# A hybrid encoder step on one core: which groups of the down projection use seven products, and where the first weights stand among the input's pieces

## The chip, the core and the metric

The kernel runs on one core of one Trainium2 chip. The time is device microseconds of one execution of the whole program. The kernel before took 2386.49 us, the median of 3 runs (2385.48 to 2387.06). One more execution was profiled: it took 2391.23 us, and its trace spans 2389.5 us from the first instruction to the last. All places below are microseconds from the start of that span.

Engine names: PE is the matrix engine (TensorE), PEld its weight loads, DVE the vector engine (VectorE), ACT the scalar engine (ScalarE), POOL is GpSimd, SP the engine whose queue issues every transfer of this kernel.

## The reference, cut to what matters

One layer of a streaming encoder, 2048 prompt tokens and 64 tokens of a running stream, model width 1024, all in float32:

```python
h = rmsnorm(x, norm1_w)
proj = h @ w_in                      # 1024 -> 2568 columns
# (A) q, k, v: causal convolution of width 4 + SiLU, gated delta rule in chunks (4 heads x 128)
# (B) 512 columns: trailing means over 2/4/8/16 frames, a 128x128 map per group, a scale
x = x + jnp.concatenate([o_delta, o_pool], axis=-1) @ w_out
h = rmsnorm(x, norm2_w)
x = x + (jax.nn.silu(h @ w_gate) * (h @ w_up)) @ w_down     # 1024 -> 2816 -> 1024
y = rmsnorm(x, normf_w)
```

It returns y for both streams and the new convolution, delta and pooling states. The change concerns the last product, `@ w_down`, and the first transfers of the program.

## The kernel before, in words

**Numbers as pairs.** Nearly every large float32 product is done on pairs: an operand is split into a high part (ACT copies it to the `F32R` type) and a low part (DVE subtracts the high part from the original). A product of two pairs is three matmuls (high·high, high·low, low·high). A split therefore costs one ACT and one DVE instruction, for weights and for activations.

**First stage** (0 to about 996 us): the tokens, 2112 in all, go through in four blocks. Block 0 takes its input as the tile pair `x0` (lines 459 and 478 to 481): two token halves (`S0`, 288 tokens each), each loaded by four transfers of two 128-row slices. `norm_apply` (line 754) turns slices into pairs, k = 0 to 7 for one half and then for the other; behind k = 1 of the first half it calls `prep()` (line 775), which loads and splits the first weight tile of `w_in` (two transfers of 256 KB). Ahead of it stand `WARM` = 12 matmuls of ones (lines 466 and 467).

**FFN stage** (from 996 us): three blocks b = 0, 1, 2 of 704 tokens, each in two halves of N2 = 352. The 2816 hidden columns are 22 tiles f of 128. For each f, `gate_up` (line 1498) makes gate and up at once in seven products of half-size operands (Strassen's scheme, 84 matmuls of 128x352); its result lies in one of three buffers `hr`. In block 0 the seven weight combinations of a tile are made by POOL, split by ACT and DVE and stored to memory (`prep_strassen`, line 577); blocks 1 and 2 load the finished pairs back.

The down projection takes the f in `FGROUPS` = (4, 4, 2, 4, 4, 4), six groups numbered 0 to 5. Group 0 follows gate/up tile 5, and groups 1 to 5 follow tiles 8, 10, 14, 18 and 21. A group is done in one of two ways:

- *plain* (`down`, line 1544): for each of 8 output tiles m and each token half, 3G matmuls, and one DVE addition of the sum in PSUM to `y`. Weights: 8 tiles of G·128 columns, each one transfer, one ACT and one DVE instruction. The activations are pairs per f and half.
- *in seven products* (`down_strassen`, line 1584): for each of 4 pairs of output tiles, 7 products of 3G/2 matmuls, each followed by a DVE addition to `y`. Weights (`prep_down`, line 611): per pair of output tiles two transfers, four POOL combinations, and four splits. The activations, two f at a time, are combined and split in `factors` (line 1561): four POOL instructions and seven splits.

Which way is set by `SDOWN` = (1, 2) (line 48) and `plain` (line 503): in block 0 all six groups are plain; in blocks 1 and 2 all are in seven products but for group 5 of block 2. The pairs of block 0 are written by `finish` (line 1516) into six places `h3t` (two tiles of three, line 1602); those of blocks 1 and 2 into tiles of the same two buffers (tag `op`), two f in each.

**What sets the order.** The program is written down in one order, and `Machine` (line 59) collects the instructions with their dependences. `issue` then writes each engine's instructions by a list planner: it keeps a modelled time per engine (costs in `cost`, line 140), and takes among the ready instructions that of the lowest rank, which is the place in the written order less a boost (`BOOST`, `HURRY`). Buffers are handed out in the plan too: an instruction whose tile has no free buffer isn't ready. On the chip each engine works through its list in order. Weight tiles are prepared up to four entries of `plan` ahead (`weights_ahead`, line 632), within the buffers: four of `wsp`, four of `wsp2` for pairs, four of `wraw` and three of `wraw2` for raw weights.

Of the kernel before, what the change touches and what calls it, by code (L numbers as in the profile page):

```python
# [12 lines left out]
F32R = mybir.dt.float32r  # L13
# [5 lines left out]
P = 128  # L19
D = 1024  # L20
KT = D // P
# [19 lines left out]
TB2 = NTOK // NB2  # L41
N2 = TB2 // 2
# [2 lines left out]
SUBS2 = ((0, N2), (N2, N2))  # L45
FGROUPS = (4, 4, 2, 4, 4, 4)

SDOWN = (1, 2)

FW = ("11", "S1", "S2", "12", "S3", "S4", "22")  # L50
FH = ("11", "T1", "T2", "21", "T3", "22", "T4")
# [302 lines left out]
def hybrid_kernel(ctx, tc, a, o):  # L354
    nc = machine = Machine(tc.nc)
# [120 lines left out]
    nw = cpool.tile([P, 3 * KT], F32, tag="nw", name="nw")  # L476
    nc.sync.dma_start(out=nw, in_=a["nw"])
    for lo, n in S0:
        for i in range(0, KT, 2):
            nc.sync.dma_start(out=x0[i // 4][:, i % 4 : i % 4 + 2, lo : lo + n],  # L480
                              in_=a["xT"][i : i + 2, :, lo : lo + n].rearrange("k p t -> p k t"))
    n1w, n2w, nfw = (nw[:, i * KT : (i + 1) * KT] for i in range(3))


# [14 lines left out]
    def halves(b, gi):  # L499

        return ((0,), (1,)) if (b, gi) == (NB2 - 1, len(groups) - 1) else ((0, 1),)

    def plain(b, gi):
        return b not in SDOWN or len(halves(b, gi)) > 1

    order = []
    for b in range(NB2):
# [246 lines left out]
    def norm_apply(B):  # L754

        hh = [bp.tile([P, 4, 2, MB], F32R, tag=f"h{i}", name=f"h{i}_{B.j}") for i in range(2)]
        B.h = [(k, hh[k // 4][:, k % 4]) for k in range(KT)]
        src = stream_x(a["xT"], "xb", B.t0)
        machine.boost = BOOST
        for lo, n in S0 if B.j == 0 else [(0, B.NB)]:  # L760
            sl = slice(lo, lo + n)
            for k in range(KT):
                w, h = n1w[:, k : k + 1], B.h[k][1]
                if B.j == 0:
                    t = from_x0(k, lo, n)
                    act(h[:, 0, sl], t, AF.Copy, scale=w)
                    stt(h[:, 1, sl], t, w, h[:, 0, sl].bitcast(F32), ALU.mult, ALU.subtract)
                else:
                    t = src(k, lo, n)
                    stt(t, t, w, B.r[:, sl], ALU.mult, ALU.mult)  # L770
                    split(h, sl, t)
                if B.j == lo == 0 and k == 1:

                    machine.boost = 2 * BOOST
                    prep()
                    machine.boost = BOOST
        machine.boost = 0
# [720 lines left out]
    def gate_up(b, f):  # L1498
# [17 lines left out]
        def finish(i, g, u):  # L1516
            e = raw[:, i]
            tt(e, e, g, ALU.mult)
            tt(e, e, u, ALU.mult)
            if b not in SDOWN:  # L1520
                split(h3t[f % 6], slice(i * N2, (i + 1) * N2), e)


        x, y, z = (psg(f"p{i}_{tag}")[:, :N2] for i in "xyz")
# [14 lines left out]
        finish(1, g2, u2)  # L1539
        add(x, "22", "T4")  # L1540
        finish(0, g1, x)
        return raw if b in SDOWN else h3t[f % 6]

    def down(b, gi, h3, ys, which, done):
        f0, G = groups[gi]
# [68 lines left out]
    for op in order:  # L1614
        b = op[1]
        if op[0] == "gu":
# [3 lines left out]
            if op == ("gu", 0, 2):  # L1620
                nxt = Chain(between(-1))
            h3[f] = gate_up(b, f)
            if b in SDOWN:
                gi = max(g for g, (f0, G) in enumerate(groups) if f0 <= f)
                if plain(b, gi):
                    if f == groups[gi][0] or f == groups[gi][0] + 2:
                        two = opool.tile([P, 2, 2, TB2], F32R, tag="op", name=f"h3l{f}", bufs=2)
                    for i in range(2):
                        split(two[:, f % 2], slice(i * N2, (i + 1) * N2), h3[f][:, i])
                    h3[f] = two[:, f % 2]  # L1630
                elif f % 2:
                    h3[f] = factors(b, f, h3.pop(f - 1), h3[f])
# [19 lines left out]


AHEAD = 3
WARM = 12
PSM = 3
BOOST = 100000

# [133 lines left out]
```

## Time and profile before

| | |
|---|---|
| median of 3 runs | 2386.49 us (2385.48 to 2387.06) |
| the profiled execution | 2391.23 us, span 2389.5 us |
| PE busy | 2347.9 us, 98% of the span, 14803 matmuls recorded |
| DVE, ACT, POOL busy | 70%, 51%, 41% of the span |
| first stage | 0 to 996 us |
| FFN block 0, 1, 2 | 996 to 1463, to 1920, to the end |

The profile's page gives the span and each engine's busy time. Matmuls are pipelined, so their recorded durations overlap: what counts is the time from one start to the next. The view of windows gives busy times, instruction counts, the granted PE clock and the rate of the transfers for any stretch; an instruction that straddles an edge is counted, and a few per cent of matmul records can be missing. In the groups of instructions a row reads: engine, operation, output<-inputs by the program's names (wsd, wsdS: pairs of the down weights; wrd, wrdt, wrdl, wrda, wrdb: raw ones; hq, h7: activations of the seven products; d and dx, dy, dz: PSUM sums of a plain group and of the seven products), shapes, count | busy us, mean ns of one | idle time ahead of it, and who ended that.

### The profile page before, as it was taken

The page shows a single profiled execution, that of the slowest core. Times are in us where ns is not written, and L with a number is a line of the kernel's source. Part 1 is how long each engine was busy: PE and PEld are TensorE (multiplying, and loading weights), DVE is VectorE, ACT ScalarE, POOL GpSimd, SP SyncE. Part 2 cuts the span into 40 slices and gives each one's busy share as a digit, 9 for nine tenths or more (in the row PEclk, how much of TensorE's full clock was granted, in tenths as well). Part 3 has the DMA queues.
Part 4 walks back from the last instruction along what each step waited for, and adds up shares of the span by engine and source line. Part 5 has one row for each costly group of instructions (what it writes and reads, how often), then busy time and mean ns, then how long its engine had stood idle before and what let it go on. Part 6 is the DMA issues. An engine that isn't in the chain of part 4 may idle for free.

```text
span 2389.5 us, 41681 instructions
## 1 busy us (share of the span) xinstructions
PE 2347.9 (98%) x14803; PEld 2183.0 (91%) x14803; DVE 1681.2 (70%) x2963; ACT 1217.8 (51%) x2746; POOL 971.1 (41%) x1146
## 2 busy tenths in 40 slices
PE   9999999999999999999999999999999999999998
PEld 8999798778887878899999999999899999999998
DVE  7999875785577786787776763767566657666466
ACT  6666654564456464574454554553333554434334
POOL 1656442554356652264332226454233464222111
PEclk9999999999999999999999999999999999999999
DMA  7644566455555575999876778976755697566763
GB/s 267 224 166 137 184 224 220 143 168 189 177 184 177 165 192 171 320 370 338 294 284 225 280 264 260 309 260 238 278 192 178 199 350 247 174 211 210 260 207 115
DMA packets 228448, 540.57 MB, mean 226 GB/s; under 512 B 28304, under 2 KB 86672, under 8 KB 228240
## 3 DMA queue, kind: packets, MB, share of 16 engines
q1 hardware_dynamic: 228240, 537.92, 66.8%
q8 instruction: 116, 1.90, 0.3%
q14 instruction: 92, 0.75, 0.1%
HBM read 389.41 MB, written 148.41 MB: 225 GB/s over the span
## 4 chain that ended last, share of the span: by engine, by line
PE 83%; DVE 8%; ACT 3%; DMA 2%; issue 2%; POOL 1%; SPq 0%; DVEq 0%; POOLq 0%; ACTq 0%
PE px L278 19%; PE pp L278 14%; PE pz L278 12%; PE py L278 10%; PE d L278 8%; PE dx L278 6%; PE dy L278 3%; PE pk_p L278 2%; PE pt_p L278 1%; PE dz L278 1%; PE gr_p L278 1%; DVE y L278 1%; PE px_p L278 1%; DVE Yqk L278 1%; PE py_p L278 1%
## 5 line engine op out<-in xcount | busy, mean ns | idle before, releaser
L278 PE MATMUL pp<-h,wsp 128*128 128x512 f32 (+1 forms) x2480 | 562.1, 366 | 3.9 <-DVE h L278 2.8
L278 PEld LDWEIGHTS pp<-h,wsp 128*128 128x128 f32 x2480 | 402.6, 190 | 52.0 <-DVE h L278 3.9
L278 POOL TENSOR_TENSOR Um_p<-Gst_p,lmask 128x256 f16<-128x256 f32 x224 | 179.0, 813 | 108.1 <-PE py_p L278 79.3
L278 PE MATMUL pz<-op,wsp 128*128 128x512 f32 (+1 forms) x960 | 216.7, 366 | 2.5 <-ACT op L278 2.0
L278 PEld LDWEIGHTS pz<-op,wsp 128*128 128x128 f32 x960 | 155.8, 190 | 22.5 <-ACT op L278 2.5
L278 PE MATMUL d<-h,wsd 128*128 128x352 f32 x1056 | 169.6, 322 | 0.0
L278 PEld LDWEIGHTS d<-h,wsd 128*128 128x128 f32 x1056 | 168.3, 188 | 0.5 <-DVE h L278 0.5
L278 DVE TENSOR_TENSOR TV_p<-TV_p,pt_p 128x512 f16<-128x512 f16 (+1 forms) x192 | 128.5, 681 | 48.4 <-PE pt_p L278 43.1
L278 PE MATMUL px<-hA,ws 128*128 128x352 f32 x792 | 141.9, 324 | 0.3 <-DMA ws<-g 0.3
L278 PE MATMUL pz<-hB,ws 128*128 128x352 f32 x792 | 139.9, 322 | 0.3 <-DMA ws<-g 0.3
L278 PE MATMUL py<-hB,wsS 128*128 128x352 f32 x792 | 139.1, 322 | 0.3 <-ACT u L278 0.3
L278 PE MATMUL px<-hBT,wsS 128*128 128x352 f32 x792 | 137.6, 322 | 1.9 <-ACT g L278 1.9
L278 PE MATMUL px<-hBT,ws 128*128 128x352 f32 x792 | 137.9, 322 | 1.5 <-DVE u L278 1.5
L278 PE MATMUL px<-hA,wsS 128*128 128x352 f32 x792 | 137.4, 322 | 0.9 <-ACT g L278 0.9
L278 POOL TENSOR_TENSOR wrS<-wr,wrS 128x512 f32<-128x512 f32 x44 | 62.9, 1430 | 185.4 <-DMA wrS<-in_wu_dram 61.2
L278 PE MATMUL py<-hA,wsS 128*128 128x352 f32 x792 | 137.4, 322 | 0.0
L278 ACT ACTIVATE hr<-g 128x352 f32<-128x352 f32 x132 | 65.7, 498 | 132.3 <-DVE g L278 131.9
L278 PEld LDWEIGHTS px<-hBT,wsS 128*128 128x128 f32 x792 | 128.2, 188 | 2.5 <-ACT g L278 2.5
L278 PEld LDWEIGHTS px<-hA,ws 128*128 128x128 f32 x792 | 129.8, 189 | 0.7 <-DMA ws<-g 0.6
L278 PEld LDWEIGHTS px<-hBT,ws 128*128 128x128 f32 x792 | 128.0, 188 | 2.3 <-DVE u L278 2.1
L278 PEld LDWEIGHTS px<-hA,wsS 128*128 128x128 f32 x792 | 128.3, 188 | 1.2 <-ACT g L278 1.2
L278 PEld LDWEIGHTS pz<-hB,ws 128*128 128x128 f32 x792 | 128.7, 188 | 0.6 <-issue 0.6
(690 smaller groups left out, 5499.8 us busy)
## 6 DMA issues: line engine op xcount, KB each, us to landing
wsS<-gS SPq DMA_DIRECT2D x176, 512.0 KB, 4.7
ws<-g SPq DMA_DIRECT2D x132, 512.0 KB, 4.7
wsp<-wnd SPq DMA_DIRECT2D x126, 512.0 KB, 3.5
gS<-wsS SPq DMA_DIRECT2D x88, 512.0 KB, 5.3
g<-ws SPq DMA_DIRECT2D x66, 512.0 KB, 5.3
wnd<-wsp SPq DMA_DIRECT2D x42, 512.0 KB, 4.7
xd<-x2d SPq DMA_DIRECT2D x96, 176.0 KB, 4.0
wrd<-in_wd_dram SPq DMA_DIRECT2D x56, 256.0 KB, 4.3
```

The source lines that it names most:

```text
L278: getattr(getattr(self.nc, op.eng), name)(*args, **kw)
```

## The change

`SDOWN` goes; a list `PLAIN` of (block, group) says which groups are plain. In block 0, group 4 (tiles 14 to 17) is now done in seven products. In blocks 1 and 2, group 2 (tiles 8 and 9) is now plain. Group 5 of block 2 stays plain through `halves`. The six places `h3t` go: in every block the pairs of a plain group are now split behind `gate_up`, into tiles of two f from the two `op` buffers, as blocks 1 and 2 did for their plain group.

At the start `x0` comes in four transfers of four slices instead of eight of two, `prep()` for the first weights is called behind k = 3 instead of k = 1, and `WARM` is 22 instead of 12.

```diff
-SDOWN = (1, 2)
+PLAIN = ((0, 0), (0, 1), (0, 2), (0, 3), (0, 5), (1, 2), (2, 2))
...
     for lo, n in S0:
-        for i in range(0, KT, 2):
-            nc.sync.dma_start(out=x0[i // 4][:, i % 4 : i % 4 + 2, lo : lo + n],
-                              in_=a["xT"][i : i + 2, :, lo : lo + n].rearrange("k p t -> p k t"))
+        for i in range(2):
+            nc.sync.dma_start(out=x0[i][:, :, lo : lo + n],
+                              in_=a["xT"][4 * i : 4 * i + 4, :, lo : lo + n].rearrange("k p t -> p k t"))
...
     def plain(b, gi):
-        return b not in SDOWN or len(halves(b, gi)) > 1
+        return (b, gi) in PLAIN or len(halves(b, gi)) > 1
...
-                if B.j == lo == 0 and k == 1:
+                if B.j == lo == 0 and k == 3:
                     machine.boost = 2 * BOOST
                     prep()
...
             tt(e, e, g, ALU.mult)
             tt(e, e, u, ALU.mult)
-            if b not in SDOWN:
-                split(h3t[f % 6], slice(i * N2, (i + 1) * N2), e)
...
-        return raw if b in SDOWN else h3t[f % 6]
+        return raw
...
-    six = [opool.tile([P, 3, 2, TB2], F32R, tag="op", name=f"h3_{i}", bufs=2) for i in range(2)]
-    h3t = [six[i // 3][:, i % 3] for i in range(6)]
...
             h3[f] = gate_up(b, f)
-            if b in SDOWN:
-                gi = max(g for g, (f0, G) in enumerate(groups) if f0 <= f)
-                if plain(b, gi):
...
+            gi = max(g for g, (f0, G) in enumerate(groups) if f0 <= f)
+            if plain(b, gi):
+                if f == groups[gi][0] or f == groups[gi][0] + 2:
+                    two = opool.tile([P, 2, 2, TB2], F32R, tag="op", name=f"h3l{f}_{b}", bufs=2)
+                for i in range(2):
+                    split(two[:, f % 2], slice(i * N2, (i + 1) * N2), h3[f][:, i])
+                h3[f] = two[:, f % 2]
+            elif f % 2:
+                h3[f] = factors(b, f, h3.pop(f - 1), h3[f])
...
-WARM = 12
+WARM = 22
```

More of the change, by code (lines that the diff above doesn't have):

```diff
@@ L1622, in hybrid_kernel @@
             h3[f] = gate_up(b, f)
-            if b in SDOWN:
-                gi = max(g for g, (f0, G) in enumerate(groups) if f0 <= f)
-                if plain(b, gi):
[L1626 to L1632, printed above, removed]
+            gi = max(g for g, (f0, G) in enumerate(groups) if f0 <= f)
[7 more added lines that the diff above has]
+                h3[f] = factors(b, f, h3.pop(f - 1), h3[f])
             if f == NF - 1 and b + 1 < NB2:
```

## The prediction, made before the changed kernel was run

> **What bounds the kernel now.** First the page: its span, and the busy time of each engine.
>
> ```profile
> span 2389.5 us, 41681 instructions
> ## 1 busy us (share of the span) xinstructions
> PE 2347.9 (98%) x14803; PEld 2183.0 (91%) x14803; DVE 1681.2 (70%) x2963; ACT 1217.8 (51%) x2746; POOL 971.1 (41%) x1146
> ```
>
> PE is busy all along, so only two things can move the end: fewer or shorter matmuls, and the places where PE waits. The profiled execution took 2391.23 us, 1.7 us more than its span; the sum below is made against it and carried over to the median, 2386.49 us. Next the view of windows, for the five kinds of down group and for the gate/up tiles around the group that changes in block 0. The columns: stretch, length, then busy time (instructions) of PE, PEld, DVE, ACT and POOL, the granted clock, and the transfers.
>
> ```profile
> 1208.02:1223.52 15.50, 15.50 (x99) 15.50 (x98) 15.26 (x27) 5.46 (x10) 5.83 (x4) 1.00 0.49 175
> 1361.12:1391.83 30.71, 30.71 (x195) 30.71 (x194) 17.34 (x28) 6.22 (x11) 8.31 (x6) 1.00 0.40 148
> 1744.42:1771.64 27.22, 27.22 (x172) 27.22 (x171) 19.62 (x39) 5.62 (x11) 8.69 (x10) 1.00 0.53 166
> 1669.60:1691.67 22.07, 18.84 (x95) 14.96 (x95) 19.87 (x42) 4.46 (x12) 8.52 (x12) 1.00 0.62 204
> 2127.34:2148.59 21.25, 19.39 (x101) 17.30 (x100) 18.57 (x40) 4.51 (x12) 6.14 (x10) 0.92 0.59 193
> 1307.54:1361.12 53.58, 53.58 (x339) 53.58 (x338) 38.27 (x60) 34.78 (x70) 14.05 (x10) 1.00 0.83 310
> 1391.67:1431.86 40.19, 40.19 (x255) 40.19 (x254) 27.73 (x44) 26.57 (x54) 9.65 (x7) 1.00 0.88 317
> ```
>
> The first three rows are dense. Group 2 of block 0, plain, is 96 matmuls (8 tiles, 2 halves, 6 each) in 15.50 us, and group 4, plain, 192 in 30.71 us: 0.160 us each. Row three, a group of four in seven products in block 1, holds 172 records less two that straddle its edges: 170 times 0.160 is 27.2 us, the row's length, so nothing is lost there. Rows four and five are the groups of two in seven products, in blocks 1 and 2. They hold 95 and 101 records, without the edges 93 and 99, that is 14.9 and 15.8 us of matmuls in 22.07 and 21.25 us. So 7.2 and 5.4 us are lost. In both, DVE is busy nearly throughout (19.87 and 18.57 us). What PE waits for there stands in the view of waits, around the one group and around the other (total, times, longest; the longest rows):
>
> ```profile
> PE px L278 <- DVE u L278: 1.1, 1, 1.1
> PE dx L278 <- DVE wsdS L278: 0.8, 1, 0.8
> ```
>
> ```profile
> PE dx L278 <- DVE y L278: 0.9, 1, 0.9
> ```
>
> All of it is DVE. The first, 1.1 us, falls at the end of gate/up tile 10, ahead of row four's stretch, while DVE already splits the group's first weights.
>
> **Blocks 1 and 2: the group of two becomes plain.** The groups of DVE instructions give the reason for the loss: mean ns is the number ahead of the second bar.
>
> ```profile
> L278 DVE TENSOR_TENSOR y<-y,dx 128x352 f32<-128x352 f32 x176 | 88.7, 516 | 33.9 <-PE dx L278 33.3
> L278 DVE TENSOR_TENSOR wsd<-wrdt,wsd 128x256 fp32r<-128x256 f32 x8 | 6.5, 812 | 0.0
> L278 DVE TENSOR_TENSOR wsdS<-wrda,wsdS 128x256 fp32r<-128x256 f32 x8 | 4.5, 559 | 0.0
> L278 DVE TENSOR_TENSOR wsdS<-wrdb,wsdS 128x256 fp32r<-128x256 f32 x8 | 3.6, 451 | 0.0
> L278 DVE TENSOR_TENSOR wsd<-wrdl,wsd 128x128 fp32r<-128x128 f32 x8 | 4.0, 506 | 0.0
> L278 DVE TENSOR_TENSOR wsd<-wrd,wsd 128x256 fp32r<-128x256 f32 x8 | 3.4, 421 | 2.3 <-DMA wr<-in_wg_dram 1.5 <-ACT wsd L278 0.9
> ```
>
> In seven products a group of two asks DVE for 28 additions of 0.516 us (14.4 us) and four times the four splits (0.812 + 0.559 + 0.451 + 0.506 = 2.33, in all 9.3 us): 23.7 us, for 84 matmuls of 13.4 us. Plain it asks for 16 additions (8.3 us) and 8 splits of 0.421 us (3.4 us): 11.7 us, for 96 matmuls of 15.4 us. PE becomes the bound again. The 16 POOL combinations of its weights and four of its activations go, and seven activation splits become four. The bytes of weights and the count of transfers stay (8 of them, through SP). A plain group of two runs dense even in block 0, where DVE is busy 15.26 of 15.50 us because it also splits gate/up weights, which blocks 1 and 2 only load; so I take no loss. Price: 12 more matmuls, +1.9 us in each block. Gain: 7.2 + 1.1 in block 1, 5.4 in block 2. Net **-6.4 and -3.5 us**. Ends: if half the loss stayed, -2.3 and -0.8; if the small waits in the gate/up tiles go too, a microsecond more.
>
> In block 2's row the clock stands at 0.92, which is 0.08 x 21.25 = 1.7 us of the 5.4. [...] The row, low just there, speaks for the waits.
>
> **Block 0: group 4 in seven products.** 168 matmuls in place of 192 at 0.160 us: -3.84 us. What else it needs:
>
> ```profile
> L278 DVE TENSOR_TENSOR wsd<-wrdt,wsd 128x512 fp32r<-128x512 f32 x36 | 35.4, 984 | 1.5 <-ACT wsd L278 0.2
> L278 DVE TENSOR_TENSOR wsdS<-wrda,wsdS 128x512 fp32r<-128x512 f32 x36 | 28.7, 798 | 1.5 <-ACT wsdS L278 0.2
> L278 DVE TENSOR_TENSOR wsdS<-wrdb,wsdS 128x512 fp32r<-128x512 f32 x36 | 29.2, 811 | 3.6 <-ACT wsdS L278 3.5
> L278 DVE TENSOR_TENSOR wsd<-wrdl,wsd 128x256 fp32r<-128x256 f32 x36 | 20.9, 581 | 1.0 <-ACT wsd L278 1.0
> L278 DVE TENSOR_TENSOR wsd<-wrd,wsd 128x512 fp32r<-128x512 f32 x56 | 43.0, 771 | 10.5 <-ACT wsd L278 8.7
> L278 DVE TENSOR_TENSOR hq<-hr,hq 128x352 fp32r<-128x352 f32 x80 | 59.7, 752 | 13.0 <-ACT hq L278 12.0
> L278 DVE TENSOR_TENSOR h<-hr,h 128x352 fp32r<-128x352 f32 x44 | 35.2, 818 | 1.2 <-ACT h L278 0.6
> L278 DVE TENSOR_TENSOR wsS<-wrS,wsS 128x512 fp32r<-128x512 f32 x88 | 72.4, 832 | 17.9 <-ACT wsS L278 16.8
> L278 POOL TENSOR_TENSOR wrda<-wrdt,wrdl 128x256 f32<-128x256 f32 x36 | 31.8, 883 | 110.9 <-DMA wrdl<-in_wd_dram 53.9 <-DVE y L278 20.3 <-DVE wsdS L278 20.2
> L278 POOL TENSOR_TENSOR q<-hr,hr 128x352 f32<-128x352 f32 x40 | 44.6, 1115 | 137.3 <-DVE hr L278 135.8
> ```
>
> DVE: 28 additions for 16 (+6.2 us), four times the four splits (0.984 + 0.798 + 0.811 + 0.581 = 3.17, 12.7 us) for 8 of 0.771 (6.2): +6.5; fourteen activation splits at 0.752 for eight at 0.818: +4.0. Together +16.7 us. POOL: 16 combinations of about 0.88 and 8 of about 1.1, +22.9 us. In the stretch from tile 15 to the end of tile 21 (the windows' rows 1307.54, 1361.12 and 1391.67, 124.4 us) DVE is busy 83.3 us and would be 100 of 120.6; POOL 32.0 and would be 54.9. Both have room, and PE hides them. In the group itself DVE has 14.4 us of additions; of the weight splits two pairs of output tiles fit into `wsp` ahead of it, two (6.4 us) fall inside, and four splits of 0.832 for gate/up tile 19: 24.1 us in 26.9. That is tight where the same group in block 1 has 19.6 in 27.2, so I put back 1.0 us of waits. Net **-2.8 us**; ends: -3.84, and +1.2 if 5 us are lost (below).
>
> **Block 0: splits behind `gate_up`, two tiles for six places.** The same number of splits, but those of tiles 4, 5, 8 and 18 now wait for a buffer `op` until groups 0, 0, 1 and 4 are through, and then stand on ACT and DVE ahead of casts for the next weights: 0.8 us of DVE each. DVE has slack for it (31% of the row from 1391.67, behind group 4). I take +0.5 us, ends 0 and +2.
>
> **The start.** ACT's and PE's rows of the timeline (start, length, what, count, wait), and two windows:
>
> ```profile
> 4.51 0.96 ACT L278 ACTIVATE h<-x,nw 128x288 fp32r<-128x288 f32 x2 [2.48 <-DMA x<-in_xT_dram]
> ```
>
> ```profile
> 8.85 5.28 ACT L278 ACTIVATE h<-x,nw 128x288 fp32r<-128x288 f32 x12 [1.17 <-DMA x<-in_xT_dram]
> ```
>
> ```profile
> 3.78 2.18 PE L278 MATMUL idle<-ones 128*128 128x128 f32 x12
> ```
>
> ```profile
> 9.99 5.34 PE L278 MATMUL pp<-h,wsp 128*128 128x288 f32 x22 [1.50 <-DVE h L278]
> ```
>
> ```profile
> 6.00:10.00 4.00, 2.03 (x9) 1.25 (x9) 1.37 (x5) 2.62 (x8) 0.00 (x0) 1.00 1.05 356
> 10.00:15.00 5.00, 5.00 (x22) 4.42 (x23) 4.78 (x12) 5.00 (x13) 0.00 (x0) 0.70 1.09 373
> ```
>
> ACT gets the first slices at 4.5 and the next at 8.85 us; from there 12 of them go at 0.44 us each, so that all 14 would be through at about 15.0. At 356 GB/s a piece of 295 KB is 0.83 us. With double pieces the first lands 0.8 us later, the place of slices 2 and 3 in the queue is taken by the second weights, slices 4 to 7 land at about 8.85 + 2 x 0.83 = 10.5 us, and the last piece four old pieces later, at 13.8; its four steps of 0.44 end at 15.6, some 0.6 us later. The ten more matmuls of ones (12 instructions took 2.18 us, so 20 take 3.6) end near 9.6 us. They cover time in which PE sat (1.5 us ahead of 9.99), but push about 2 us of real work behind them, into a stretch where PE is paced by DVE. The clock there was 0.70, which costs nothing as long as DVE paces. I take **+0.5 us**, ends -0.6 and +2.0. The four transfers saved on SP are not on the path.
>
> **Sum.** -6.4 - 3.5 - 2.8 + 0.5 + 0.5 = -11.7 us: 2391.23 becomes 2379.5, and the median 2386.49 becomes 2374.8; I say **2375**.
>
> **Rivals.** (1) *Block 0 gives the gain back.* DVE shares time with POOL: one split can take twice its median (min/median/max, ns):
>
> ```profile
> L278 DVE TENSOR_TENSOR wsdS<-wrdb,wsdS x44: 411/686/1429, 1537.5 to 2292.6; 128x512 fp32r<-128x512 f32 x36, 128x256 fp32r<-128x256 f32 x8
> ```
>
> If the 22.9 us of added POOL work held DVE up as long, DVE would want 123 of 120.6 us; and counted over the group alone with all its splits and tile 19's seven (27.1 + 5.8 us), it wants 6 us more than PE's 26.9. The two groups of two lost 0.5 to 0.8 of their excess of 10.3 us. That is up to 5 us of waits, 4 more than I took: -7.7, **2379**. [...] Against: block 0 runs dense with DVE at 98% in group 2.
>
> (2) *Slower: ACT stands before a full buffer.* In blocks 1 and 2 ACT waits for the release of `op` by the last product:
>
> ```profile
> ACT hq L278 <- PE dx L278: 72.3, 7, 11.9
> ```
>
> Seven waits of 10 us. There it casts only the down weights. In block 0 the gate/up weights come on top, and find their buffers during the same groups:
>
> ```profile
> ACT ws L278 <- PE d L278: 39.6, 12, 7.0
> ```
>
> If the planner puts the split of tile 4, 8 or 18 into ACT's list ahead of those casts, the next gate/up tile finds no weights. Three places (behind groups 0, 1, 4) at up to 10 us: at 6 us each +18 - 11.7 = +6, **2393**. It decides from 3.9 us a place. Against: the planner issues what is ready in its own time, and the casts are ready before the release.
>
> (3) *No change: the list is written anew from the start.* Larger pieces are booked in the planner by another rate, so that the order of the first stage shifts. Its waits:
>
> ```profile
> PE pc L278 <- POOL ext L278: 2.7, 1, 2.7
> ```
>
> That is the longest; four new ones like it would eat the sum, -11.7 + 10.8: **2386**. Against: PE's work there stays the same, and orders change for better as often.
>
> (4) *The loss isn't DVE's rate* but the late activations, and plain groups of two lose it too: blocks 1 and 2 then pay 1.9 us each for matmuls, -2.8 + 3.8 + 1 = +2, **2388.5**. Against: DVE's busy time in those windows.
>
> **How the numbers follow.** Forecast 0.74 (its own range 2370 to 2378.5), rival 1 0.11, rival 2 0.05, rival 3 0.07, rival 4 0.03. A difference of 0.2%, 4.8 us, is about what a measurement of this kernel tells from none. Faster takes the forecast and nearly all of rival 1: 0.84; the same takes most of rivals 3 and 4: 0.10; slower 0.06. The range holds the forecast with its ends and rival 1, and the order's luck of 3 us either way: **2368 to 2382**.
>
> **What would show it.** In the changed profile: group 2 of blocks 1 and 2 as 96 matmuls `d` in 15.4 us with no wait of PE; group 4 of block 0 in 27 to 28 us, and behind it no wait for `ws` or `wsS` over 1 us; DVE near 100 us from tile 15 to tile 21; the first dense matmuls within 1 us of before. It is wrong if PE waits for DVE or ACT in block 0, or if the first stage ends more than 3 us from 996.

## The result, and the profile after

The changed kernel takes 2383.15 us (median of 20 runs, 2380.11 to 2387.28) where the kernel before, run beside it, takes 2388.36 (20 runs, 2385.48 to 2391.84): a ratio of 0.9978, 95% interval 0.9972 to 0.9984. That is 5.2 us faster, where 11.7 were forecast, and 2383 lies above the range given (2368 to 2382). The forecast was reckoned from 2386.49, the median of three runs, which is 1.9 us below the 2388.36 of these 20; so 1.9 of the 8.3 us between 2374.8 and 2383.15 belong to neither kernel.

The profiled execution took 2383.12 us, its span is 2380.5 us. From its page:

```profile
PE 2344.3 (98%) x14823; PEld 2184.7 (92%) x14823; DVE 1674.3 (70%) x2943; ACT 1215.7 (51%) x2738; POOL 967.2 (41%) x1130
```

PE's busy time hardly tells anything: a wait that shortens and a matmul that goes look alike in it. So the two programs are laid side by side by stage. The kernel before was profiled a second time for that (2387.89 us, span 2386.1), because its first profiled execution, 2391.23, lies 2.9 us above the median of its own runs; the second lies within 0.5 us of it. The cuts are the first gate/up matmul of a tile: of block 0, of block 1, of the tiles ahead of and behind the group of two in block 1, the same in block 2, and the end; two stretches that differ by 0.1 us are left out. First the kernel before, second execution (stretch, length, then busy time and instructions of PE, PEld, DVE, ACT, POOL, the granted clock, and the transfers):

```profile
0.00:994.08 994.08, 976.25 (x6308) 824.85 (x6308) 752.66 (x1409) 568.33 (x1409) 465.42 (x650) 1.00 0.59 191
994.08:1461.80 467.72, 465.17 (x2910) 463.59 (x2909) 330.65 (x512) 243.06 (x489) 186.86 (x149) 1.00 0.81 296
1638.00:1701.80 63.80, 59.69 (x350) 55.55 (x350) 41.92 (x81) 22.20 (x51) 23.14 (x30) 1.00 0.77 281
1701.80:2095.80 394.00, 390.46 (x2430) 388.09 (x2430) 257.45 (x440) 179.28 (x371) 154.12 (x162) 1.00 0.69 229
2095.80:2156.00 60.20, 57.85 (x350) 55.46 (x350) 36.41 (x73) 22.24 (x51) 14.00 (x20) 1.00 0.65 227
```

and the changed kernel:

```profile
0.00:996.55 996.55, 979.23 (x6327) 828.29 (x6328) 753.39 (x1410) 567.40 (x1409) 462.68 (x650) 0.99 0.58 191
996.55:1464.18 467.63, 462.69 (x2886) 459.78 (x2884) 350.74 (x537) 249.08 (x503) 208.18 (x173) 1.00 0.81 295
1640.30:1697.80 57.50, 57.50 (x362) 57.50 (x361) 30.55 (x58) 18.01 (x39) 13.34 (x14) 1.00 0.91 318
1697.80:2092.80 395.00, 391.38 (x2431) 388.05 (x2430) 258.20 (x440) 179.24 (x372) 149.88 (x156) 1.00 0.68 228
2092.80:2150.30 57.50, 57.50 (x361) 57.50 (x361) 24.44 (x50) 18.02 (x39) 4.77 (x6) 1.00 0.70 231
```

Row by row: the first stage is 2.5 us longer; block 0 is as long as before (-0.1), although it has 24 matmuls fewer (2886 for 2910); the two stretches with the groups of two are 6.3 and 2.7 us shorter and dense (PE busy 57.50 of 57.50, with twelve and eleven more records of matmuls); the long stretch between them takes 1.0 more, which is no more than two executions of one kernel differ by there (395.1 us in the first execution of the kernel before, from 1703.2 to 2098.3, against 394.0 in the second). Together 5.6 us of span. So one part of the change works, one does nothing, and one costs.

What PE waits for in block 0, from tile 15 to block 1's first tile (1308.04 to 1464.18), by the view of waits; in both executions of the kernel before, this view names no wait of PE in the same stretch:

```profile
PE px L278 <- DVE u L278: 1.8, 1, 1.8
PE dx L278 <- DVE y L278: 0.8, 2, 0.6
PE d L278 <- DVE h3l L278: 0.2, 1, 0.2
```

The first of these is one wait, at the end of tile 16 (start, length, what, count, wait):

```profile
1335.83 1.39 PE L278 MATMUL px<-hBT,ws 128*128 128x352 f32 x7 [1.76 <-DVE u L278]
```

### The profile page after: what moved, and what is told of

It reads as the page before. It is cut to its first block, busy times and chain, and to the rows that moved or that the text cites. A ratio compares the mean times of both kernels' runs of the same rounds, so it can differ in the third digit from the quotient of the medians.

```text
span 2380.5 us, 41651 instructions
## 1 busy us (share of the span) xinstructions
PE 2344.3 (98%) x14823; PEld 2184.7 (92%) x14823; DVE 1674.3 (70%) x2943; ACT 1215.7 (51%) x2738; POOL 967.2 (41%) x1130
## 4 chain that ended last, share of the span: by engine, by line
PE 81%; DVE 9%; ACT 3%; DMA 3%; issue 2%; SPq 1%; POOL 1%; DVEq 0%; POOLq 0%; ACTq 0%
PE px L278 19%; PE pp L278 14%; PE pz L278 11%; PE py L278 9%; PE d L278 8%; PE dx L278 5%; PE dy L278 3%; PE pk_p L278 2%; PE pt_p L278 1%; PE dz L278 1%; PE gr_p L278 1%; PE px_p L278 1%; DVE Yqk L278 1%; PE py_p L278 1%; ACT E L278 1%
## 5 line engine op out<-in xcount | busy, mean ns | idle before, releaser
L278 PE MATMUL d<-h3l,wsd 128*128 128x352 f32 x1248 | 201.3, 322 | 0.2 <-DVE h3l L278 0.2
L278 PEld LDWEIGHTS d<-h3l,wsd 128*128 128x128 f32 x1248 | 199.1, 188 | 1.2 <-DVE h3l L278 0.7
L278 PEld LDWEIGHTS py<-hB,wsS 128*128 128x128 f32 x792 | 128.6, 188 | 0.4 <-ACT u L278 0.4
```

Source lines behind the costliest of these rows:

```text
L278: getattr(getattr(self.nc, op.eng), name)(*args, **kw)
```

## The experiments

Below, "the stretch" is always that from tile 15 of block 0 to block 1's first tile: 155.3 us in both executions before, 156.1 after. It scatters: in the six profiles below with groups 4 and 5 of block 0 plain it takes 155.3 to 156.1, and two of these, of one kernel, have 156.1 and 155.8. A difference under 1 us in it tells nothing. In the kernels of the first group one part of the change is undone, or done alone.

### One part at a time

*Block 0 all plain*, the rest as changed:

```diff
-PLAIN = ((0, 0), (0, 1), (0, 2), (0, 3), (0, 5), (1, 2), (2, 2))
+PLAIN = ((0, 0), (0, 1), (0, 2), (0, 3), (0, 4), (0, 5), (1, 2), (2, 2))
```

> The changed kernel with group 4 of block 0 plain again; all else as changed. Theory A (block 0's group gains nothing: its 3.84 us of matmuls come back as waits of PE for DVE, whose splits are stretched while POOL runs): as the changed kernel within 1 us, near 2383; the stretch from gate/up tile 15 to tile 21 in block 0 takes 124.3 us as before and holds no wait of PE for DVE. Theory B (the prediction's price, a gain of 2.8 us): 2.8 us slower than the changed kernel, near 2386.

Measured: 2384.29 us (11 runs), ratio 0.9982 [0.9974, 0.9991], stretch 155.6.

*The old start* (eight pieces of x, first weights behind k = 1, 12 matmuls of ones), the rest as changed:

```diff
-                if B.j == lo == 0 and k == 3:
+                if B.j == lo == 0 and k == 1:
...
-WARM = 22
+WARM = 12
```

> The changed kernel with the start as before: eight pieces of x, first weights behind two slices, 12 matmuls of ones. Theory A (the start costs what was predicted, 0.5 us): 0 to 1 us faster than the changed kernel, and the FFN stage begins near 996.0 in place of 996.6. Theory C (the missing 6 us went into the start and the first stage's order): 3 us or more faster, near 2380.

Measured: 2381.39 us (5 runs), ratio 0.9964 [0.9951, 0.9976], stretch 156.8.

*The groups of two in seven products again*, the rest as changed:

```diff
-PLAIN = ((0, 0), (0, 1), (0, 2), (0, 3), (0, 5), (1, 2), (2, 2))
+PLAIN = ((0, 0), (0, 1), (0, 2), (0, 3), (0, 5))
```

> The changed kernel with group 2 of blocks 1 and 2 in seven products again. Theory A (the groups of two gave 9.9 us in the profiled pair, 1.7 of it a halved clock that not every run has): 7 to 9 us slower than the changed kernel, 2390 to 2392. Theory D (the median run of the kernel before loses less there than its profiled run, about 5 us in the two groups): 5 us slower, near 2388.

Measured: 2390.43 us (11 runs), ratio 1.0011 [1.0002, 1.0020], stretch 155.4 with group 4 in seven products as in the changed kernel. Without the plain groups of two nothing of the gain is left.

*The groups of two plain alone* (block 0 all plain, old start):

> The kernel before with one part of the change alone: group 2 of blocks 1 and 2 plain (and the pairs of block 0 split behind gate_up into two tiles, which the list of plain groups brings with it). Theory A: 7 to 9 us faster than before, 2379 to 2381, and faster than the changed kernel by up to 1 us. Theory B: 9.4 us faster, near 2379, and 2.3 us slower than the changed kernel was forecast. Theory D: 5 us faster, near 2383.

Measured: 2380.68 us (5 runs), ratio 0.9964 [0.9950, 0.9977]; this one edit does more than the whole change. Measured once more:

> The version with only the groups of two plain, old start, block 0 all plain, once more beside the others. By theory A 2380 to 2382, within 2 us of the version with DVE's combinations; by the prediction's price of block 0 that version would lie 2.8 us lower.

2380.70 us (8 runs), ratio 0.9973 [0.9962, 0.9983]. The stretch in this execution, with group 4 plain:

```profile
1307.30:1463.10 155.80, 155.71 (x975) 154.96 (x974) 97.36 (x155) 81.53 (x167) 61.32 (x56) 1.00 0.75 269
```

What follows: the plain groups of two are worth 7.3 us (2390.43 less 2383.15 with them undone; 7.3 and 7.4 done alone, against the kernel before run beside them: 2387.94 and 2388.06). Group 4 of block 0 in seven products is worth nothing: -1.1 us with the new start, +0.7 with the old one, both within what these intervals leave open; the stretch says the same, 156.1, 156.8 and 155.4 in the three kernels that have it so, 155.3 to 156.1 with the group plain. So of the theories on record B, the prediction's price of block 0, falls, and A, that it gains nothing, stands; C, that the start costs, has 1.8 us in it by one pair (2383.15 less 2381.39) and 3.6 by the other, with block 0 all plain (2384.29 less 2380.68).

*The kernel before, profiled again:*

> The kernel before, profiled a second time. Theory D (the first profiled execution lost more in the groups of two than the kernel usually does, 1.7 us of it in a window at half the clock in block 2's group): no window at half the clock in that group, the stretch from block 2's tile 9 to its tile 12 takes 59 to 60 us instead of 61.0, and the profiled execution comes out 1 to 4 us under 2391. If the loss is the same each time, the stretch is 61 again and the time 2391.

It took 2387.89 us; the group's stretch in block 2 took 60.2 us against 61.0 in the first execution (tile starts at 2098.3 and 2159.3), with the clock at 1.00 where the first had 0.92 in the group's own row. So the execution on which the prediction's sum was made lost 0.8 us more there, which is theory D in kind. In size it falls: of the group's loss of 5.4 us 4.6 are there again, and undoing the groups of two cost 7.3 us, where D expected 5.

### Why block 0 gains nothing

*The combinations left out.* In group 4 of block 0 the splits read the loaded weights and the raw activations, and POOL's 24 combinations are gone, so y of the first 704 tokens leaves them out. Old start. The core of the edit:

```diff
-        s31, s24 = (wtiles(f"d{i}", True)[0]() for i in "ab")
-        gt = nc.gpsimd.tensor_tensor
+        if bare:
+            s31, s24 = top, low
+            gt = lambda **kw: None
```

> The changed kernel with the start as before, and in block 0's group 4 no POOL work: the 16 combinations of its weights and the 8 of its activations are left out, and the splits take the raw tiles instead, as many as before (so the y of the first 704 tokens is wrong in part). Theory A (POOL's work stretches DVE's splits, and that makes PE wait): the activation splits of block 0 take 0.52 us each in place of up to 1.6, PE no longer waits for DVE behind gate/up tile 16, and the stretch from tile 15 to block 1 takes 152.5 us, 3.8 less than the 156.3 of the kernel with POOL's work. Theory E (DVE's own count of instructions is what fills block 0): the waits stay, 156 us.

Measured: 2375.74 us (5 runs), ratio 0.9949 [0.9937, 0.9962]. The windows, of the kernel with the old start and POOL's combinations first, then of this one:

```profile
1307.40:1464.20 156.80, 153.83 (x950) 151.23 (x949) 119.54 (x181) 88.57 (x181) 85.68 (x80) 1.00 0.74 268
```

```profile
1305.10:1457.30 152.20, 152.02 (x949) 151.16 (x949) 110.79 (x181) 88.98 (x181) 59.89 (x54) 1.00 0.77 276
```

With the same 181 instructions, DVE is busy 8.8 us less when POOL does not work beside it, and the stretch is 4.6 us shorter: 3.1 under the 155.3 of the kernel before, near the 3.84 us of the matmuls. So the saving is there when the combinations are gone. But this version also takes two of the activation splits behind tile 15 out of their place, as is shown below, so the 4.6 us are not POOL's work alone.

*Group 5 instead of group 4* in seven products, else the groups of two alone:

> The start as before, groups of two plain, and in block 0 group 5 in seven products in place of group 4. Behind it block 1 begins, whose gate/up weights are loaded ready, so DVE is less asked (13.4 of 31 us in the group before) but POOL is busy with the next activations (30 of 31 us). Theory A (it is the meeting of POOL and DVE that costs): as the kernel with the groups of two alone or slower, near 2381. Theory E (DVE's count): the 3.8 us come through, near 2377.

Measured: 2383.86 us (11 runs), ratio 0.9983 [0.9974, 0.9992]. The stretch fell to 154.0 us, but block 1's first tile behind it takes 18.5 us instead of 13.4:

```profile
1457.80:1476.30 18.50, 16.51 (x92) 15.96 (x91) 3.12 (x6) 11.33 (x26) 17.18 (x21) 0.91 1.04 397
```

POOL is busy 17.18 of those 18.50 us and DVE only 3.12, so what runs late there is more likely POOL's own work; the granted clock of 0.91 (0.09 x 18.5, an estimated 1.7 us) is another part, and no run isolates either. Another group is no way out.

*Combinations on DVE*, as far as `factors` makes them (old start):

```diff
     def factors(b, f, u, v):
...
-        gt = nc.gpsimd.tensor_tensor
+        gt = nc.gpsimd.tensor_tensor if b else nc.vector.tensor_tensor
```

> The changed kernel with the old start, and in block 0's group 4 the 16 weight combinations and 8 activation combinations computed by DVE instead of POOL; nothing is left out. Theory A (POOL's added work stretches DVE's splits, and PE waits for those): DVE takes the 24 combinations itself, at about 0.5 us each 12 us more of its own, but its splits beside them are short again (0.5 to 0.7 us), so the stretch from tile 15 to block 1's first tile falls from 156.8 us to 153 to 155, and the time to some 2 us under the 2381 of the old start with POOL: 2378 to 2380. Theory E (block 0 is filled by DVE's own count of work): 12 us more of DVE's work make it longer, 157 us and more, 2382 to 2385.

Measured: 2380.81 us (8 runs), ratio 0.9969 [0.9958, 0.9979], stretch 155.8. The edit was smaller than its expectation says: it moves the 8 combinations of activations only; the 16 of weights stayed on POOL. It agrees with neither theory and settles nothing. So, with the weights' too:

```diff
     def prep_down(m, f0, G, first=False):
...
-        gt = nc.gpsimd.tensor_tensor
+        gt = nc.vector.tensor_tensor if first else nc.gpsimd.tensor_tensor
```

> The changed kernel with the old start, and all 24 combinations of block 0's group 4 (16 of weights, 8 of activations) computed by DVE instead of POOL; nothing is left out. (The earlier run with this aim moved the 8 of the activations only.) Theory A (POOL's work and DVE's splits share time): DVE's busy time from tile 15 to block 1's first tile stays near the 119.5 us that it has with POOL, because its 24 additional instructions replace the time lost beside POOL, and the stretch takes 153 to 155 us. Theory E (the amount of work): DVE's busy time goes up by 10 us or more, to 130, and the stretch to 157 or more. Theory F (the splits wait for late combinations): on DVE they come sooner, 153 to 155 too.

Measured: 2378.10 us (4 runs), ratio 0.9957 [0.9942, 0.9972]; the whole reference is computed, and it is the fastest such version here. By the stretch it is 2.1 us shorter than the same kernel with POOL (154.7 against 156.8; against the two others with this group in seven products, 156.1 and 155.4, it is 1.4 and 0.7) and about 1 us shorter than the groups of two alone (155.8 and 156.1), which is near the scatter; the intervals of the three overlap.

```profile
1303.70:1458.40 154.70, 152.49 (x950) 151.17 (x950) 117.57 (x205) 88.78 (x181) 61.49 (x56) 1.00 0.76 271
```

DVE has 24 instructions more and is busy 2 us *less* than with POOL's help (117.57 against 119.54). That speaks for theory A and against E, which wanted 130. The groups of DVE instructions in the stretch show where the time is. With the old start and POOL (mean ns ahead of the second bar):

```profile
L278 DVE TENSOR_TENSOR y<-y,dx 128x352 f32<-128x352 f32 x16 | 7.9, 511 | 0.7 <-PE dx L278 0.7
L278 DVE TENSOR_TENSOR hq<-q,hq 128x352 fp32r<-128x352 f32 x4 | 5.2, 1304 | 0.0
```

and with all combinations on DVE:

```profile
L278 DVE TENSOR_TENSOR y<-y,dx 128x352 f32<-128x352 f32 x16 | 8.0, 512 | 0.6 <-PE dx L278 0.5
L278 DVE TENSOR_TENSOR q<-hr,hr 128x352 f32<-128x352 f32 x4 | 2.1, 517 | 0.0
L278 DVE TENSOR_TENSOR hq<-q,hq 128x352 fp32r<-128x352 f32 x4 | 2.1, 517 | 0.0
```

The same split `hq<-q,hq` takes 1304 ns beside POOL and 517 alone. The addition `y<-y,dx`, one of whose operands is PSUM, takes 511 and 512. A combination of activations costs 517 ns on DVE; on POOL the same one takes 1138 and the split beside it takes 790 longer. At the end of tile 16 this version wins little: PE still waits 0.5 us for `g` and 0.4 for `u` there, and the four combinations now stand in DVE's own list ahead of `u`.

*POOL's work kept, its results read by nobody* (old start; the splits read raw weights and activations, so that no split waits for POOL):

```diff
+        if first:
+            s31, s24 = top, low
         for i, (nms, raw) in enumerate(((("11", "12"), top), (("S3", "S1"), s31), ...
...
+        if b == 0:
+            t2, t3, t4 = v[:, 1], u[:, 1], v[:, 0]
```

> The changed kernel with the old start; in block 0's group 4 POOL computes all its 24 combinations from the same operands into buffers that nobody reads, and the splits read the loaded weights and the raw activations instead, so that POOL's work stays and no split waits for it. The combinations are thereby left out of the computation: y of the first 704 tokens is partly wrong. Theory A: DVE's splits are as long as with POOL (busy time near 119 us), and the stretch stays at 155.5 to 157. Theory F: it falls to 152 to 153, as without the combinations. In between, both have a part.

Measured: 2377.90 us (4 runs), ratio 0.9955 [0.9940, 0.9970].

```profile
1306.40:1460.40 154.00, 153.14 (x950) 151.23 (x949) 118.85 (x181) 88.00 (x181) 83.71 (x78) 1.00 0.77 273
```

```profile
L278 DVE TENSOR_TENSOR h<-hr,hq 128x352 fp32r<-128x352 f32 x2 | 2.7, 1333 | 0.0
```

A split that waits for nothing from POOL still takes 1333 ns (the same one takes 518 where POOL's combinations are left out), and DVE is busy 118.85 us: the split is longer with POOL at work beside it, not through waiting. But the stretch falls to 154.0, between what theory A (155.5 to 157) and theory F (152 to 153) expected of this run. That doesn't show that the other 2.8 us are waits for late combinations, for the edit also changes DVE's list. In the changed kernel two of the seven splits of a pair of tiles read combinations that need the second tile, or that are made behind one that does; here they read the first tile alone, and the planner puts them ahead. Four splits instead of six then stand between the last instruction of tile 15's activations, `hr<-hr,u`, and `u`:

```profile
1322.28 0.53 DVE L278 TENSOR_TENSOR hr<-hr,u 128x352 f32<-128x352 f32 x1
1330.66 0.51 DVE L278 TENSOR_TENSOR u<-px,u 128x352 f32<-128x352 f32 x1
```

From the one to the other it is 8.4 us here and 11.1 in the changed kernel (timeline below), which is two splits of 1.3 us. The kernel without any combinations and the one without those of the activations also have four splits there. So the longer splits beside POOL and their number at that place are shown; a part of waiting isn't.

*Only one kind of combination left out* (old start; y of the first 704 tokens leaves them out): the weights',

> The changed kernel with the old start and the 16 combinations of weights of block 0's group 4 left out (the splits read the loaded weights; y of the first 704 tokens is partly wrong), those of the activations kept. They are 14 of POOL's 23 us. By theory A the stretch falls by about 14/23 of the 4.6 us, to 154; if the activations' combinations alone do the harm, which sit around tile 16 where PE waited 1.8 us, it stays at 156.

2379.61 us (5 runs), ratio 0.9965 [0.9952, 0.9978]:

```profile
1306.90:1461.20 154.30, 152.51 (x950) 151.15 (x949) 117.20 (x181) 89.24 (x181) 69.23 (x62) 1.00 0.76 272
```

and the activations':

> The changed kernel with the old start and the 8 combinations of activations of block 0's group 4 left out (the splits read the raw activations; y of the first 704 tokens is partly wrong), those of the weights kept. By theory A the stretch falls by 9/23 of the 4.6 us, to 155; if the activations' combinations alone do the harm, to 152.5.

2375.59 us (4 runs), ratio 0.9951 [0.9934, 0.9967]:

```profile
1304.80:1457.30 152.50, 152.24 (x949) 151.20 (x949) 112.12 (x181) 87.84 (x181) 76.54 (x72) 1.00 0.78 275
```

Taking away the eight combinations of activations gives back 4.3 of the 4.6 us (with two splits moved ahead), those of the weights 2.5 (with the list at tile 16 as it was, and PE's wait for `u` still 1.6 us); the two overlap. Once the others are gone, what the 16 of the weights cost, 0.3 us, is under the scatter, though they are two thirds of POOL's instructions. What the eight do is seen in the changed kernel's DVE timeline behind tile 15 (start, length):

```profile
1324.15 0.53 DVE L278 TENSOR_TENSOR hr<-hr,u 128x352 f32<-128x352 f32 x1
...
1326.38 1.26 DVE L278 TENSOR_TENSOR hq<-hr,hq 128x352 fp32r<-128x352 f32 x1
1327.57 1.27 DVE L278 TENSOR_TENSOR hq<-q,hq 128x352 fp32r<-128x352 f32 x1
1328.76 1.27 DVE L278 TENSOR_TENSOR hq<-hr,hq 128x352 fp32r<-128x352 f32 x1
1329.95 1.61 DVE L278 TENSOR_TENSOR hq<-q,hq 128x352 fp32r<-128x352 f32 x1
...
1333.12 1.61 DVE L278 TENSOR_TENSOR h<-q,hq 128x352 fp32r<-128x352 f32 x1
...
1335.26 0.51 DVE L278 TENSOR_TENSOR u<-px,u 128x352 f32<-128x352 f32 x1
```

and on POOL:

```profile
1324.75 1.16 POOL L278 TENSOR_TENSOR q<-hr,hr 128x352 f32<-128x352 f32 x1 [2.74 <-DVE hr L278]
1325.99 1.28 POOL L278 TENSOR_TENSOR hr<-hr 128x352 f32<-128x352 f32 x1
1327.35 1.11 POOL L278 TENSOR_TENSOR q<-hr,hr 128x352 f32<-128x352 f32 x1
1328.53 1.11 POOL L278 TENSOR_TENSOR q<-hr,q 128x352 f32<-128x352 f32 x1
1329.61 1.57 POOL L278 TENSOR_TENSOR wrS<-wr,wrS 128x512 f32<-128x512 f32 x1
1332.73 1.62 POOL L278 TENSOR_TENSOR wrS<-wr,wrS 128x512 f32<-128x512 f32 x1 [1.55 <-DVE wsS L278]
```

Split and combination alternate: each of these five splits ends 0.37 to 0.39 us after the POOL instruction beside it, the last two after combinations of gate/up weights (`wrS`). A sixth split stands in the first gap; it began before POOL's first combination and takes 0.52 us. All six stand in DVE's list ahead of `u`, which frees the PSUM buffer for the next product. No row of DVE between `hr<-hr,u` and `u` has an idle time, so DVE waits for nothing there, not for a late combination either; it is the list that is long. `u` starts at 1335.26, and PE, waiting for it, stands 1.8 us.

### The start

*More ones alone* (the groups of two alone, with `WARM` 22), *larger pieces with moved weights alone* (the block-0-plain kernel with `WARM` 12), and *larger pieces with the weights' transfers behind k = 1 as before*:

> The kernel with the groups of two alone and 22 matmuls of ones in place of 12, the rest of the start as before. If the ones cost what the start costs (real matmuls pushed behind them): 1 to 3 us slower than with 12, near 2382.5, and the sums of squares of the first half end about a microsecond later. If the larger pieces do it: as with 12, near 2380.7.

> The kernel with the groups of two alone and the larger pieces of x with the first weights behind four slices, but 12 matmuls of ones. If the pieces cost what the start costs: 1 to 3 us slower than without them, near 2382.5. If the ones do it: near 2380.7. If it is the order of the first stage, which either may shift: both this kernel and the one with more ones are slower, by amounts that fall between 27 and 996 us and not ahead of 27 us.

> The version with only the groups of two plain, with the larger pieces of x, but the first weights' transfers behind the second slice as before, and 12 matmuls of ones. With the weights moved too it took 2383.6, without either 2380.7. If the pieces cost (their later landing puts the sums of squares behind the casts), it stays at 2383 to 2384; if the moved weights cost, it falls to 2381.

Measured: 2382.80 us (11 runs), ratio 0.9979 [0.9970, 0.9988]; 2383.56 (10 runs), 0.9974 [0.9965, 0.9983]; 2382.91 (10 runs), 0.9976 [0.9967, 0.9986]. Against the 2380.7 of the old start each costs about 2 us, but the intervals overlap, so the medians alone decide nothing. The lengths of the first stage in the profiles are sharper, if like is compared with like: the clock is halved near 41 us, for 3.4 us in some executions and for 6.8 in others, and in most of them for 3.4 us more near 886 us (granted 0.50 from 42.7 to 46.2 and from 885.8 to 889.3 us in the first execution of the kernel before, from 43.8 to 47.3 and from 886.9 to 890.4 in the changed kernel's; last part). With 6.8 us and the second window, the old start has 994.8, 995.0, 995.2 and 995.3; larger pieces have 997.6 with 12 matmuls of ones and 997.4 with 22. (The other three executions with larger pieces, the changed kernel's among them, have 994.7, 996.6 and 997.7, with windows like none of the old start.) With 3.4 us and the second window, the old start has 993.2 to 995.1, and the ones alone 995.6. So the larger pieces cost about 2.4 us. What the ones cost can't be told from the scatter, and beside the larger pieces they cost nothing; the place of the weights' transfers can't be told either. A like pair of rows, the groups of two alone, and the same with larger pieces and moved weights:

```profile
0.00:995.27 995.27, 977.16 (x6307) 825.03 (x6308) 752.43 (x1409) 568.33 (x1409) 465.34 (x650) 0.99 0.59 191
```

```profile
0.00:997.59 997.59, 977.98 (x6307) 825.96 (x6308) 753.95 (x1410) 568.03 (x1409) 463.10 (x650) 0.99 0.59 190
```

Where the 2.4 us begin: the timeline of the groups of two alone (another execution), then of the changed kernel. The last sum of squares of each token half is the row `sq7n`.

```profile
8.20 5.21 ACT L278 ACTIVATE h<-x,nw 128x288 fp32r<-128x288 f32 x12
17.09 0.65 PE L278 MATMUL rpn<-sq7n,ones 128*128 128x288 f32 x2
24.92 0.65 PE L278 MATMUL rpn<-sq7n,ones 128*128 128x288 f32 x2
```

```profile
9.25 5.36 ACT L278 ACTIVATE h<-x,nw 128x288 fp32r<-128x288 f32 x12 [0.23 <-DMA x<-in_xT_dram]
18.56 0.65 PE L278 MATMUL rpn<-sq7n,ones 128*128 128x288 f32 x2
26.53 0.65 PE L278 MATMUL rpn<-sq7n,ones 128*128 128x288 f32 x2
```

The last slices of `h` are through at 14.6 us in both (9.25 + 5.36 here; there two slices follow the twelve). But of ACT's eight squares of x, three come ahead of 14.5 us with the small pieces and one with the large; seven instead of five stand behind `h`, and the last sum of squares comes at 18.56 instead of 17.09. In all five executions with larger pieces it comes at 17.8 to 18.6, and in eleven with the old start at 16.4 to 17.1 (the first execution of the kernel before, 18.2, had its clock halved, granted 0.50, from 12.0 to 15.5 us); in the second half at 25.7 to 26.5 against 24.2 to 24.9. So, by the means, 1.5 to 1.7 of the 2.4 us are lost ahead of 27 us, with the squares. Where the rest is lost isn't shown.

## Why the prediction came out wrong

**Groups of two: right in mechanism and nearly in size.** 96 matmuls `d` in 15.5 us with no wait of PE was forecast, and that is what runs:

```profile
1669.07:1684.57 15.50, 15.50 (x99) 15.50 (x98) 12.57 (x22) 1.24 (x3) 9.13 (x10) 1.00 0.88 274
2121.53:2137.03 15.50, 15.50 (x99) 15.50 (x98) 9.88 (x20) 1.24 (x3) 1.44 (x2) 1.00 0.73 237
```

Rival 4 (the plain groups lose it too) falls with these rows. The term was -6.4 and -3.5. Against the execution from which it was read it is met: there the two stretches take 64.05 us (from 1639.12 to 1703.17) and 61.02, now 57.5 each:

```profile
2098.25:2159.27 61.02, 59.16 (x350) 57.07 (x349) 36.35 (x73) 22.18 (x50) 13.96 (x20) 0.97 0.65 223
```

Against the second execution, with 63.80 and 60.20, it is -6.3 and -2.7. So the mis-sized part is "5.4 us are lost" in block 2: 0.8 of it belonged to the one execution with a half clock there. The prediction counted that window as 1.7 and put it down to the waits ("The row, low just there, speaks for the waits"). The waits were there in the second execution too (one of 0.93 us, where the first had 0.92), and the clock stayed at 1.00, so the waits alone don't bring the window. Without these 1.7 the term would have been -1.8; the measured -2.7 lies midway.

Done alone, the plain groups bring 7.3 us by the medians and not 9. In the two profiles of that kernel the long stretch between the groups takes 397.5 and 397.1 us, where the kernel before has 395.1 and 394.0; why, no run isolates. And the two executions of the kernel before differ by 3.4 us of span, 1.8 of it in the first stage and 1.1 in these two groups, so a sum made against the slower one can't be carried to the median whole.

**Block 0: the step that failed.** "Both have room, and PE hides them" is where it goes wrong. Matmuls were right (-3.84 and as many fewer records), POOL's +22.9 us nearly too (by the stretch's rows with the old start, group 4 plain and in seven products: 61.3 to 85.7). But DVE went up by more than the 16.7 us that were counted: from 97.4 to 119.5 it is 22.2, of which the same instructions without POOL's combinations are 13.4 (110.8). DVE is at 76% of the stretch even so. An average share with room in it hid most of these 22 us, but not the 4.6 by which the stretch exceeds 155.3 less 3.84 (156.1 for 151.5), since much of the added work comes in one lump, at one place of DVE's list, ahead of the instruction that frees PSUM. In the group itself the sum held: 27 to 28 us were forecast, and in the changed kernel it takes 27.55. With 164 matmuls inside (26.2 us) that holds 1.3 us of waits, where 1.0 was put back.

```profile
1366.61:1394.16 27.55, 26.74 (x166) 26.03 (x164) 25.94 (x45) 9.74 (x18) 12.19 (x11) 1.00 0.45 156
```

The largest single piece of the loss, 1.8 us of PE's waiting, lies ahead of it, at the end of tile 16, where the prediction only counted shares. Rival 1 named a cause that the runs show (DVE sharing time with POOL) and priced it at 5 us of waits in all, near the 4.6 measured; it had a chance of 0.11. The 2.3 us forecast net of the splits became 0.1 in block 0. How the 4.6 us divide between the longer splits and the number of splits that stand in that one place is open, since each version that takes the activations' combinations from POOL changes both, or adds to DVE's list. The traces show the lengthening at the split `hq<-q,hq`, whose inputs both lie in SBUF, 1304 ns beside POOL and 517 alone, and none at the addition `y<-y,dx`, which has one in SBUF and one in PSUM: 511 and 512. Who waits for the longer splits is what decided, and that is read from the timeline.

**Splits behind `gate_up`.** PE waits once in the stretch for `h3l`, 0.2 us, and ACT never stands before `op` so that PE notices. +0.5 was taken; with group 4 plain, where this is the only change in block 0, the stretch is 0 to 0.8 us longer than before. Rival 2 didn't come.

**The start: mis-sized.** +0.5 with ends -0.6 and +2.0; about 2.4 came. The step that failed is the one on ACT's slices, "some 0.6 us later". The last slice of `h` was to end at 15.6 instead of 15.0 and ends at 14.6, no later than with the groups of two alone. But the prediction followed `h` alone: the sums of squares, on the same engine, were not in the sum, and they come 1.5 us later. Rival 3 (the list of the first stage written anew) has a part here, since the place of the squares in ACT's list changed. The price was a quarter of its 10.8.

Together, by the two executions that lie near their medians: +2.5, -0.1, -0.1, -6.3, +1.0, -2.7, +0.1: -5.6 us of span. Of the 6.1 us missing to 11.7, 2.0 are the start, 2.2 block 0, 0.9 the groups of two, and 1.0 the scatter of the stretch between them.

## What to carry to other kernels

Added work on an engine with slack is free only if nothing urgent stands behind it in that engine's list: look up which instruction it delays and who waits for that one, and read slack at that place, not as a share of a stage (in the changed kernel DVE was busy 119.92 of the stretch's 156.14 us, and PE stood 1.8 us for `u`). Where POOL makes what DVE reads next, compare with doing it on DVE: here 24 more instructions on DVE left it busy for less time (117.57 us against 119.54), and the stretch became 0.7 to 2.1 us shorter than in the three kernels with POOL. (The kernel itself, 2378.1 us against 2381.4, is not told apart from it by the intervals.) Before a version that leaves work out is read as the price of that work, compare the engines' lists: here it also moved two splits. And make a sum against an execution that lies near the median of its runs, or profile twice; here the first one was 2.9 us above it.

## What the runs showed of the hardware that was not expected

The granted clock falls to 0.50 for some 3.4 us at a time, and not in each execution. Ahead of these windows PE had waited 1.50 us (the window from 12.0 us), 2.72 (42.7), 1.12 and 1.29 (885.8) and 0.92 and 0.29 (2141.9) in the first execution of the kernel before, and 2.85 (43.8), 1.66 (723.0) and 2.17 (886.9) in the changed kernel's. The first execution of the kernel before has the wait ahead of 723 too, 1.65 us, and its clock stays at 1.00 there; and of the two executions of that kernel only the first has a window in block 2's group (the second has 1.00 from 2122 to 2147). Behind a wait of 2.06 us and one of 0.55, in the kernel with the old start (a PE row, then the window after it):

```profile
883.54 0.71 PE L278 MATMUL px_p<-TV_p,F_p 128*128 128x128 f32 x4 [2.06 <-DVE F_p L278]
```

```profile
885.50:888.90 3.40, 3.35 (x8) 2.67 (x9) 3.40 (x6) 1.85 (x4) 1.19 (x2) 0.54 0.73 207
```

The kernel with all combinations on DVE waits 2.0 us near the same place, at 882.4, and keeps its clock:

```profile
PE pz L278 <- ACT op L278: 2.0, 1, 2.0
```

```profile
884.40:888.00 3.60, 3.60 (x22) 2.85 (x21) 3.12 (x8) 1.31 (x3) 1.96 (x2) 1.00 0.86 259
```

With the old start, the first stage ends at 992.0 to 992.2 us where this window is missing and the one near 41 us lasts 3.4 us, and at 993.2 to 995.1 where only the later window is added. Half the clock for 3.4 us accounts for at most 1.7 us of this (3.4 x 0.5), so the later window isn't all of the difference. The runs of one kernel spread by up to 9 us (the kernel before in one comparison, 2385.96 to 2394.74), and differences of 2 us between two kernels, as in the start, have to be read by stage, with the windows of half clock alike. What decides which execution has a window isn't shown by any run.
